# Modulation batches placed behind the next group of small matmuls, with a shorter gap to their loads and other metering of the convolution taps

## The chip, the cores and the metric

The kernel runs on one core of a Trainium2 chip. The core has a matrix engine (TensorE, PE in the rows, its weight loads PEld), a vector engine (VectorE, DVE), a scalar engine (ScalarE, ACT), GpSimd (POOL) and SyncE (SP), which here issues most DMAs. Each engine works through its own list of instructions in order; semaphores tie the lists together. The metric is the time of one execution in microseconds, the median of several runs.

## The reference

One layer of a hybrid backbone, over 128 context tokens and 256 latent tokens with 2048 channels, all float32:

```python
sh1, sc1, g1, sh2, sc2, g2 = modulation(cond, lp["w_mod"], lp["b_mod"])   # silu(cond) @ w_mod + b_mod
hcur = x * (1 + sc1) + sh1
q, k, v, u, gt, z, xbc, dt = jnp.split(hcur @ lp["w_in"], cuts, axis=-1)
o_a = attention(q, k, v)                  # 16 heads; latent: neighbourhood plus context keys
o_b = conformer_conv(u, gt, ...)          # silu(LN(dwconv31(u * sigmoid(gt))))
o_c, h_state = ssd_mixer(z, xbc, dt, ...) # dwconv5, chunked scan in both directions, gate, RMSNorm
mix = jnp.concatenate([o_a, o_b, o_c], axis=-1) @ lp["w_out"]
x = layer_norm(ALPHA * x + g1 * mix, ...)
hcur = x * (1 + sc2) + sh2
ff = conv_ffn(hcur, lp["w_up"], ..., lp["w_down"])
x = layer_norm(ALPHA * x + g2 * ff, ...)
```

The six modulation vectors are products of a 2048-vector (two of them: context and latent) with a 2048 x 12288 matrix. Four of the six belong to the stage that the change touches or lie near it: gate 1 and scale 2 are made on TensorE ("modulation batches" below), shift 2 on VectorE.

## The kernel before

**Large matmuls.** A float32 weight piece is loaded (`wpiece`), ScalarE rounds it to a high part `whi` (line 229) and VectorE subtracts to get the low part `wlo` (line 230, "weight split"). Each product is three matmuls, high by high, high by low and low by high: lines 454 to 456 (`tok_mm`, tokens on the output partitions) and 460 to 462 (`chan_mm`, channels on the output partitions). There are four `whi` and four `wlo` buffers of half a piece each.

**The stage.** After the first input projection comes a stage with a hand-made order on TensorE: line 993 opens a `manual_schedule` for that engine alone, so TensorE's list is the order in which the code emits; the lists of the other engines are set by a scheduler from program order, priorities and its own estimates. The large matmuls of the stage are, in order: z and dt (`phase_zd`), values (`phase_v`), eight head pairs of keys and queries (`qk_tile`), and the first 512 output columns (`wo_group(0, ...)`).

**The planner.** Between them, groups of small matmuls are put in by a planner, `_Flow`. It keeps a clock in estimated microseconds. `tick(us)` is called after each few large matmuls and moves the clock; generators that are due are then run up to their next `yield cost, delay`: the clock moves by `cost` and the generator comes back `delay` later. The generators of the stage are:
- `tok_gen`: transposes of the convolved channels (lines 418, 424);
- `dt_gen`: the time steps of the scan. Line 498 makes two cumulative sums, line 499 copies each to `cs` on VectorE, lines 501 and 503 go on from there;
- `ssm_gen`: the scan (lines 541, 579, 584, 592, transposes on 608);
- `attn_gen`: per head pair and block of queries, scores (lines 698, 701, 703), then one step later the transposes of the softmax (line 726) and a step later the values (line 739), copied by line 742;
- `conv_ln_gen`: the LayerNorm of the 31-wide convolution (lines 372, 385), once the convolution is done;
- `mod2_gen`: the modulation batches. 64 pieces, three at a time (`most`), in 22 batches, each followed by its `gap`. A batch loads three pieces of 128 x 1024 floats (512 KB each, `mod2_load`) into the three `v` buffers, waits `gap` on the planner's clock, and then makes four matmuls of 32 columns of weights for each piece (line 786). They are `gm<-v,cond` in the rows: `cond` is loaded as weights in 32-column tiles, `v` streams through;
- `sh2_gen`: the products for shift 2 on VectorE.

The 31 taps of the convolution (line 358, and 354 for the first of a channel tile; 124 in all) are the planner's background `bg`: `tick` adds `us * rate` to a credit and emits taps while the credit lasts. `rate` is 0.45 up to the end of `phase_v` and 0.7 from then on. The taps run on VectorE.

Of the kernel before, what the change touches and what calls it, by code (L numbers as in the profile page):

```python
# [47 lines left out]
class _Flow:  # L48
# [2 lines left out]

    def __init__(self, step):
        self.now, self.last, self.n, self.q, self.bg, self.credit, self.step = 0.0, 0.0, 0, [], [], 0.0, step
        self.rate = 0.0

    def add(self, delay, gen):
        self.n += 1
# [2 lines left out]
    def run(self):  # L60
        self.last = self.now
        while self.q and self.q[0][0] <= self.now:
            gen = heappop(self.q)[2]
            said = next(gen, None)
            if said is not None:
                self.now += said[0]
                self.add(said[1], gen)

    def tick(self, us):
        self.now += us  # L70
# [12 lines left out]
    def drain(self):  # L83
        while self.bg:
            self.bg.pop(0)[0]()
        while self.q:
            self.advance()


# [10 lines left out]
def _build(tc, ctx, a):  # L100
# [16 lines left out]
    flow = _Flow(1.5)  # L117
# [232 lines left out]
    def conv31_steps(i):  # L350
        def first():
            do_glu(i)
            cvo[i] = t_t(399)
            V.tensor_scalar(out=cvo[i][:, :399], in0=glu[i][:, 0:399], scalar1=P_("conv_w", 31 * i),
                            scalar2=P_("conv_b", i), op0=ALU.mult, op1=ALU.add)

        def tap(j):
            V.scalar_tensor_tensor(out=cvo[i][:, :399], in0=glu[i][:, j:j + 399], scalar=P_("conv_w", 31 * i + j),
                                   in1=cvo[i][:, :399], op0=ALU.mult, op1=ALU.add)

        return [(first, 1.2)] + [(lambda j=j: tap(j), 0.63) for j in range(1, 31)]
# [3 lines left out]
    def conv_ln_gen():  # L365
        while flow.bg:
            yield 0.0, 1.0
        yield 0.0, 3.0
        n = 399
        ps = at_t()  # L370
        for i in range(4):
            PE.matmul(ps[:, :n], ones, cvo[i][:, :n], start=i == 0, stop=i == 3)
        mu = g_t()
        S.activation(out=mu[:, :n], in_=ps[:, :n], func=AF.Copy, scale=1.0 / 512)
        yield 2.7, 3.0
        sqs = []
        for i in range(4):
            V.tensor_tensor(out=cvo[i][:, :n], in0=cvo[i][:, :n], in1=mu[:, :n], op=ALU.subtract)
            sq = g_t()
            S.activation(out=sq[:, :n], in_=cvo[i][:, :n], func=AF.Square)  # L380
            sqs.append(sq)
            yield 0.0, 2.0
        sm = at_t()
        for i in range(4):
            PE.matmul(sm[:, :n], ones, sqs[i][:, :n], start=i == 0, stop=i == 3)
        rs = g_t()
        S.activation(out=rs[:, :n], in_=sm[:, :n], func=AF.Sqrt, scale=1.0 / 512, bias=eps_t)
        yield 2.7, 0.0
        for c0, c1 in ((0, 133), (133, 266), (266, 399)):
            yield 0.0, 3.0  # L390
            V.reciprocal(out=rs[:, c0:c1], in_=rs[:, c0:c1])
        for i in range(4):
            yield 0.0, 2.0
            V.tensor_tensor(out=cvo[i][:, :n], in0=cvo[i][:, :n], in1=rs[:, :n], op=ALU.mult)
        for i in range(4):
            for c0, c1 in CSEG:
                S.activation(out=cvo[i][:, c0:c1], in_=cvo[i][:, c0:c1], func=AF.Silu,
                             scale=P_("cln_g", i), bias=P_("cln_b", i))
            ready.add(8 + i)
# [8 lines left out]
    def do_conv5(i):  # L408
        o = t_t(386)
        taps(o, xbc_raw[i], lambda j: ("sconv_w", 5 * i + j), 5, P_("sconv_b", i), 386)  # L410
        S.activation(out=o, in_=o, func=AF.Silu)
        xact[i] = o

    def tok_gen():
        for c in range(3):
            ps = at_t()
            for i in range(4):
                PE.transpose(ps[:, 128 * i:128 * i + 128], xact[i][:, OFF[c]:OFF[c] + 128], ident)
            xtok[c] = m_t()
            S.copy(out=xtok[c], in_=ps)  # L420
            yield 0.5, 1.5
            ps = at_t()
            for i in range(2):
                PE.transpose(ps[:, 128 * i:128 * i + 128], xact[4 + i][:, OFF[c]:OFF[c] + 128], ident)
            btok[c] = sbt([128, 256], "btok", 3)
            S.copy(out=btok[c], in_=ps[:, :256])
            yield 0.3, 1.5
        ready.add("tok")
# [187 lines left out]
    def ssm_gen():  # L616
        while not {"tok", "dt"} <= ready:
            yield 0.0, 1.0
        yield from state_steps(0, 0)
        yield from state_steps(0, 1)  # L620
        yield from chunk_steps(0)
        load_state()
        yield from state_steps(1, 0)
        yield from state_steps(2, 1)
        yield from chunk_steps(1)
        yield from chunk_steps(2)
        ready.add("ssm")
        ready.update(range(12, 16))
# [147 lines left out]
    def mod2_start(g):  # L776
        gS[g] = gm_t()

    def mod2_load(i):
        g, half, k = i // 32, i // 16 % 2, i % 16  # L780
        return load(a["wm2"][g, half, k], 1024, v_t().rearrange("p a b -> p (a b)"))

    def mod2_piece(i, raw):
        g, half, k = i // 32, i // 16 % 2, i % 16
        for j in range(4):
            PE.matmul(gS[g][32 * j:32 * j + 32, 256 * half:256 * half + 256], cond[:, k, :],
                      raw[:, 256 * j:256 * j + 256], start=k == 0, stop=k == KC - 1)
# [5 lines left out]
    def mod2_end(g):  # L793
        ps = gS.pop(g)
        vv = v_t()
        sm, bg = vv[:, 0, :], vv[:, 1, :]
        if g == 0:
            pinned(bg, a["bgate"])
            with tc.high_priority(offset=HP):
                V.tensor_tensor(out=sm, in0=ps, in1=bg, op=ALU.add)  # L800
            gd[g] = dr.tile([2, D], F32, tag=f"gd{g}", name=nm("gd"))
            for j in range(4):
                G.dma_start(out=gd[g][:, 512 * j:512 * j + 512], in_=sm[32 * j:32 * j + 2, :])
            return
        V.tensor_copy(out=sm, in_=ps)
        yield 0.0, 2.0
        pt = at_t()
        for b in range(4):
            PE.transpose(pt[:, 128 * b:128 * b + 128], sm[:, 128 * b:128 * b + 128], ident)
        pv = pt.rearrange("p (b j c) -> p j b c", b=4, j=4)[:, :, :, 0:2]  # L810
        V.tensor_tensor(out=s2.rearrange("p (j b) c -> p j b c", j=4), in0=pv,
                        in1=bc(b2p.rearrange("p (j b) -> p j b", j=4), 3, 2), op=ALU.add)
        yield 0.5, 1.0

    def mod2_gen(most, gap):
        i = 0
        while i < 64:
            n = min(most, 32 - i % 32)
            raws = [mod2_load(j) for j in range(i, i + n)]
            yield 0.0, gap  # L820
            if i % 32 == 0:
                mod2_start(i // 32)
            for j, raw in enumerate(raws):
                mod2_piece(i + j, raw)
            i += n
            yield 0.45 + 0.43 * n, 0.0
            if i % 32 == 0:
                yield from mod2_end((i - 1) // 32)
# [52 lines left out]
    def sh2_gen(gap):  # L881
        while "ssm" not in ready:
            yield 0.0, 1.0
        for _ in range(3):
            sh2_load()
            yield 0.0, gap
        while "stop" not in ready:
            sh2_step()
            yield 0.0, gap
# [103 lines left out]
    with tc.manual_schedule(engines={mybir.EngineType.PE}):  # L993
        for i in range(8):
            do_conv5(i)
        for i in range(4):
            flow.bg += conv31_steps(i)
        flow.rate = 0.45
        flow.add(30.0, tok_gen())
        flow.add(0.0, mod2_gen(3, 12.0))  # L1000
        flow.add(40.0, conv_ln_gen())
        flow.add(30.0, ssm_gen())
        flow.add(50.0, attn_gen())
        flow.add(60.0, sh2_gen(4.0))
        phase_zd()
        flow.add(0.0, dt_gen())
        phase_v()
        flow.rate = 0.7
        for hp in range(8):
            k = qk_tile(0, hp)  # L1010
            qk[hp] = (qk_tile(1, hp), k)
        ps = [mm_t() for _ in range(3)]
        for k in ORDER[:12]:
            cat_split(k)
        wo_group(0, ps, cat_split, lambda last: flow.tick(2.09))
        ready.add("stop")
        flow.drain()
        gb = mix_rows(0)
        for t in range(3):
            mix_evac(t, 0, 0, 512, ps[t], gb)  # L1020
# [333 lines left out]
```

## Time and profile before

| | us |
|---|---|
| median of 3 runs | 1811.7 (1810.92 to 1812.44) |
| the profiled execution | 1812.03 |
| its span, first to last instruction | 1810.2 |
| TensorE busy | 1780.8 (98%) |
| VectorE busy | 1213.4 (67%) |
| ScalarE busy | 774.6 (43%) |

The page tells the busy time of each engine, and the trace behind it each instruction with its start, its duration and what it waited for. On TensorE the starts are what counts: matmuls overlap at their ends, so the distance between two starts is the time that a matmul costs. In the order of time, a row ends with idle time in brackets where the engine stood still before it, and the name of what ended that.

### The profile page before, as it was taken

The numbers are of one execution on the slowest core, as the hardware profiler recorded it, in microseconds if no ns is written. First come the engines' busy times: TensorE is split into PE (matmuls) and PEld (weight loads), VectorE is DVE, ScalarE is ACT, GpSimd is POOL, SyncE is SP. The second block draws the span as 40 slices with busy tenths as digits, with TensorE's granted clock in tenths as the row PEclk, the third lists the DMA queues.
The fourth block names the chain that finished last, engine by engine and source line by source line (L and its number), as shares of the span: only waits on it lengthen the run. The fifth ranks groups of instructions, "written<-read, shape, count | busy, mean of one in ns | idle before, by whom it ended". The sixth has DMA issues, their size and how long they took to land. (4 is left out here: it accounts for less than half of the span.)

```text
span 1810.2 us, 28844 instructions
## 1 busy us (share of the span) xinstructions
PE 1780.8 (98%) x10794; PEld 1620.9 (90%) x10794; DVE 1213.4 (67%) x2591; ACT 774.6 (43%) x1466; POOL 62.6 (3%) x149
## 2 busy tenths in 40 slices
PE   7999999999999999999999999999999999999998
PEld 6888997888887899999889999989999988999987
DVE  3866899885999566667535667535676544766577
ACT  4222454656764246444433444323444323444434
POOL 0000001110001000000000000000000000000000
PEclk9999999999999999999999999999999999999999
DMA  8999457766999452445444454444544544444454
GB/s 317 310 322 321 148 199 254 241 210 204 356 344 336 138 162 86 142 140 161 130 129 152 151 175 162 135 128 134 175 163 145 158 123 140 163 146 153 121 152 139
DMA packets 113259, 337.75 MB, mean 187 GB/s; under 512 B 13096, under 2 KB 17672, under 8 KB 113120
## 3 DMA queue, kind: packets, MB, share of 16 engines
q1 hardware_dynamic: 105888, 311.65, 52.2%
q0 software_dynamic: 7232, 24.28, 4.5%
q8 instruction: 84, 1.38, 0.3%
q14 instruction: 55, 0.45, 0.1%
HBM read 331.08 MB, written 4.79 MB: 186 GB/s over the span
## 5 line engine op out<-in xcount | busy, mean ns | idle before, releaser
L229 ACT CAST whi<-raw 128x512 fp32r<-128x512 f32 (+1 forms) x755 | 467.5, 620 | 869.1 <-PE mm L461 291.4
L230 DVE TENSOR_TENSOR wlo<-raw,whi 128x512 fp32r<-128x512 f32 (+1 forms) x755 | 519.8, 689 | 428.3 <-ACT whi L229 426.4
L460 PE MATMUL mm<-hl,whi 128*128 128x384 f32 x1245 | 425.2, 342 | 1.4 <-ACT whi L229 1.1
L461 PE MATMUL mm<-hl,whi 128*128 128x384 f32 x1245 | 419.5, 337 | 0.0
L462 PE MATMUL mm<-hl,wlo 128*128 128x384 f32 x1245 | 418.8, 336 | 0.0
L460 PEld LDWEIGHTS mm<-hl,whi 128*128 128x128 f32 x1245 | 233.6, 188 | 12.2 <-issue 5.5
L461 PEld LDWEIGHTS mm<-hl,whi 128*128 128x128 f32 x1245 | 233.8, 188 | 0.6 <-DVE wlo L230 0.2
L462 PEld LDWEIGHTS mm<-hl,wlo 128*128 128x128 f32 x1245 | 233.7, 188 | 0.0
L460 PE MATMUL sc<-hl,whi 128*128 128x384 f32 x659 | 222.8, 338 | 0.0
L461 PE MATMUL sc<-hl,whi 128*128 128x384 f32 x659 | 221.8, 337 | 0.0
L462 PE MATMUL sc<-hl,wlo 128*128 128x384 f32 x659 | 221.7, 336 | 0.0
L460 PEld LDWEIGHTS sc<-hl,whi 128*128 128x128 f32 x659 | 123.6, 188 | 2.9 <-ACT whi L229 1.6
L461 PEld LDWEIGHTS sc<-hl,whi 128*128 128x128 f32 x659 | 123.7, 188 | 0.1
L462 PEld LDWEIGHTS sc<-hl,wlo 128*128 128x128 f32 x659 | 123.7, 188 | 0.0
L843 DVE SCALAR_TENSOR_TENSOR junk<-raw,gb 128x512 bf16<-128x512 f32 x128 | 87.6, 684 | 51.1 <-DMA raw<-wg 50.9
L454 PE MATMUL mm<-whi,hl 128*128 128x512 f32 (+2 forms) x293 | 101.2, 345 | 0.1
L456 PE MATMUL mm<-whi,hl 128*128 128x512 f32 (+2 forms) x293 | 99.4, 339 | 0.0
L455 PE MATMUL mm<-wlo,hl 128*128 128x512 f32 (+2 forms) x293 | 99.3, 339 | 0.0
L456 PE MATMUL mm<-whi,t 128*128 128x512 f32 (+1 forms) x232 | 89.6, 386 | 0.0
L454 PE MATMUL mm<-whi,t 128*128 128x512 f32 (+1 forms) x232 | 89.6, 386 | 0.0
L843 DVE SCALAR_TENSOR_TENSOR junk<-m,m 128x512 bf16<-128x512 f32 x128 | 87.9, 687 | 2.5 <-DMA m<-wsh 0.6
L455 PE MATMUL mm<-wlo,t 128*128 128x512 f32 (+1 forms) x232 | 89.5, 386 | 0.0
(353 smaller groups left out, 2474.8 us busy)
## 6 DMA issues: line engine op xcount, KB each, us to landing
raw<-wu SPq DMA_DIRECT2D x176, 512.0 KB, 3.5
raw<-wd SPq DMA_DIRECT2D x79, 512.0 KB, 3.6
m<-wm SPq DMA_DIRECT2D x128, 256.0 KB, 5.7
v<-wm SPq DMA_DIRECT2D x64, 512.0 KB, 6.4
raw<-wA SPq DMA_DIRECT2D x32, 512.0 KB, 5.4
raw<-wqk SPq DMA_DIRECT2D x32, 512.0 KB, 4.5
m<-wsh SPq DMA_DIRECT2D x64, 256.0 KB, 6.1
raw<-wo SPq DMA_DIRECT2D x32, 512.0 KB, 4.7
```

The source lines that it names most:

```text
L229: S.copy(out=hi[:, :w], in_=rw)
L230: V.tensor_tensor(out=lo[:, :w], in0=rw, in1=hi[:, :w].bitcast(F32), op=ALU.subtract)
L454: PE.matmul(ps[:, :n], A, hi[:, w0:w0 + n], start=k == 0, stop=False)
L455: PE.matmul(ps[:, :n], A, lo[:, w0:w0 + n], start=False, stop=False)
L456: PE.matmul(ps[:, :n], B, hi[:, w0:w0 + n], start=False, stop=k == last)
L460: PE.matmul(ps[:, :T], A, hh[k], start=k == k0, stop=False)
L461: PE.matmul(ps[:, :T], A, hl[k], start=False, stop=False)
L462: PE.matmul(ps[:, :T], B, hh[k], start=False, stop=k == k1)
L843: V.scalar_tensor_tensor(out=j, in0=w, scalar=1.0, in1=cbc[s], op0=ALU.mult, op1=ALU.mult, accum_out=macc[:, 16 * s + kt, kq:kq + 1])
```

## The change

Three things. (1) A generator may now say `None` as its delay. Then it is put on a list `behind`, and is run as soon as another generator has emitted a group with a cost above zero. `mod2_gen` says so once, after its gap, so that a batch's matmuls stand directly behind the next group of small matmuls in TensorE's list. `drain` empties the list at the end of the stage. (2) The gap between a batch's loads and its matmuls is 5 instead of 12 on the planner's clock. (3) The rate of the taps is 0.25 instead of 0.45 up to the end of `phase_v`, and 0.85 instead of 0.7 after it. No matmul, load or vector instruction is added or dropped.

```diff
--- before.py
+++ after.py
@@ -51,7 +51,7 @@
 
     def __init__(self, step):
         self.now, self.last, self.n, self.q, self.bg, self.credit, self.step = 0.0, 0.0, 0, [], [], 0.0, step
-        self.rate = 0.0
+        self.rate, self.behind = 0.0, []
 
     def add(self, delay, gen):
         self.n += 1
@@ -64,7 +64,14 @@
             said = next(gen, None)
             if said is not None:
                 self.now += said[0]
-                self.add(said[1], gen)
+                if said[1] is None:
+                    self.behind.append(gen)
+                else:
+                    self.add(said[1], gen)
+                if said[0] > 0:
+                    for other in self.behind:
+                        self.add(-1.0, other)
+                    self.behind = []
 
     def tick(self, us):
         self.now += us
@@ -83,7 +90,9 @@
     def drain(self):
         while self.bg:
             self.bg.pop(0)[0]()
-        while self.q:
+        while self.q or self.behind:
+            while self.behind:
+                self.add(0.0, self.behind.pop())
             self.advance()
 
 
@@ -818,6 +827,7 @@
             n = min(most, 32 - i % 32)
             raws = [mod2_load(j) for j in range(i, i + n)]
             yield 0.0, gap
+            yield 0.0, None
             if i % 32 == 0:
                 mod2_start(i // 32)
             for j, raw in enumerate(raws):
@@ -995,9 +1005,9 @@
             do_conv5(i)
         for i in range(4):
             flow.bg += conv31_steps(i)
-        flow.rate = 0.45
+        flow.rate = 0.25
         flow.add(30.0, tok_gen())
-        flow.add(0.0, mod2_gen(3, 12.0))
+        flow.add(0.0, mod2_gen(3, 5.0))
         flow.add(40.0, conv_ln_gen())
         flow.add(30.0, ssm_gen())
         flow.add(50.0, attn_gen())
@@ -1005,7 +1015,7 @@
         phase_zd()
         flow.add(0.0, dt_gen())
         phase_v()
-        flow.rate = 0.7
+        flow.rate = 0.85
         for hp in range(8):
             k = qk_tile(0, hp)
             qk[hp] = (qk_tile(1, hp), k)
```

Lines behind the class move by 9 in the changed kernel, and by 10 behind `mod2_gen`'s new line: line 786 is 795 there, 499 is 508, 742 is 751.

TensorE, values (`phase_v`): the two cumulative sums of the time steps (`at<-dA`) and what stands around them. Before:

```order
L456 MATMUL mm_3087<-whi_3245,hl_87 128x512
L498 MATMUL at_3263<-dA_95,cons_66 128x24 x2
L454 MATMUL sc_3085<-whi_3249,hl_86 128x512
L455 MATMUL sc_3085<-wlo_3250,hl_86 128x512
L456 MATMUL sc_3085<-whi_3249,hl_87 128x512
```

and in the changed kernel:

```order
L465 MATMUL mm_3057<-whi_3204,hl_87 128x512
L507 MATMUL at_3222<-dA_95,cons_66 128x24 x2
L795 MATMUL gm_2967<-v_3122,cond_63 32x256 x4
L795 MATMUL gm_2967<-v_3124,cond_63 32x256 x4
L795 MATMUL gm_2967<-v_3126,cond_63 32x256 x4
L463 MATMUL sc_3055<-whi_3208,hl_86 128x512
L464 MATMUL sc_3055<-wlo_3209,hl_86 128x512
L465 MATMUL sc_3055<-whi_3208,hl_87 128x512
```

A batch of three pieces now stands between the cumulative sums and the nine large matmuls that come before line 501 (510); before there were the nine alone.

VectorE, the same place: from the first copy of `cs` to just behind the second. `wlo` is a weight split, `t<-g,par,t` a tap, `vt` the addition of a finished group of values. Before:

```order
L499 COPY cs_89<-at_3263 128x3x8
L358 SCALAR_TENSOR_TENSOR t_3231<-g_3225,par_68,t_3231 128x399
L230 TENSOR_TENSOR wlo_3359<-raw_3356,whi_3358 128x512
L667 TENSOR_TENSOR vt_326<-vt_326,sc_3085 128x512
L667 TENSOR_TENSOR vt_327<-vt_327,sc_3086 128x512
L667 TENSOR_TENSOR vt_328<-vt_328,mm_3087 128x512
L230 TENSOR_TENSOR wlo_3363<-raw_3356,whi_3362 128x512
L499 COPY cs_89<-at_3263 128x3x8
```

and in the changed kernel:

```order
L508 COPY cs_89<-at_3222 128x3x8
L367 SCALAR_TENSOR_TENSOR t_3500<-g_3494,par_68,t_3500 128x399
L239 TENSOR_TENSOR wlo_3310<-raw_3307,whi_3309 128x512
L508 COPY cs_89<-at_3222 128x3x8
L367 SCALAR_TENSOR_TENSOR t_3500<-g_3494,par_68,t_3500 128x399
```

The second copy now comes ahead of the three additions and of one of the two splits.

ScalarE, values of the sixth head pair: `t<-at` is the copy of line 742 (751), `hl<-t` the rounding of a finished input of the output projection, `qk<-mm` a finished query tile. Before:

```order
L245 CAST hl_6126<-t_3699 128x128
L229 CAST whi_6166<-raw_6164 128x512
L245 CAST hl_6126<-t_3231 128x256
L245 CAST hl_6126<-t_3699 128x256
L245 CAST hl_6126<-t_4296 128x256
L245 CAST hl_6126<-t_2632 128x256
L742 COPY t_5977<-at_5962 128x384
L728 COPY pt_5981<-at_5979 128x128
```

and in the changed kernel:

```order
L725 ACTIVATE p_5864<-p_5864,sm_5863 128x128
L238 CAST whi_5940<-raw_5934 128x512
L238 CAST whi_6021<-raw_6019 128x512
L238 CAST whi_6025<-raw_6019 128x512
L691 COPY qk_5930<-mm_5797 128x384
L751 COPY t_5962<-at_5947 128x384
L737 COPY pt_5966<-at_5964 128x128
```

The roundings of `hl` no longer stand ahead of the copy.

## Rows read from the trace of the kernel before

**Rows 1.** The page, part 1: busy time of the engines, share, instructions.

```profile
PE 1780.8 (98%) x10794; PEld 1620.9 (90%) x10794; DVE 1213.4 (67%) x2591; ACT 774.6 (43%) x1466; POOL 62.6 (3%) x149
```

**Rows 2.** Stretches: us; PE, PEld, DVE, ACT, POOL busy (instructions), clock, DMA.

```profile
260.00:290.00 30.00, 27.98 (x182) 22.03 (x180) 29.81 (x69) 14.51 (x28) 0.51 (x1) 1.00 0.60 205
290.00:330.00 40.00, 40.00 (x249) 34.62 (x241) 39.43 (x68) 15.85 (x35) 7.24 (x12) 1.00 0.79 272
330.00:380.00 50.00, 47.43 (x364) 41.05 (x364) 36.34 (x80) 31.25 (x81) 6.18 (x10) 1.00 0.62 211
380.00:430.00 50.00, 49.22 (x369) 42.11 (x370) 37.76 (x80) 35.27 (x90) 9.80 (x16) 1.00 0.70 229
```

**Rows 3.** TensorE's waits for others: total us, times, longest.

```profile
PE at L726 <- ACT t L742: 3.9, 7, 1.1
```

**Rows 4.** TensorE in order of time: a batch alone. Start, us, instruction.

```profile
478.21 0.33 PE L461 MATMUL mm<-hl,whi 128*128 128x384 f32 x1
478.38 0.34 PE L462 MATMUL mm<-hl,wlo 128*128 128x384 f32 x1
478.65 1.50 PE L786 MATMUL gm<-v,cond 128*32 128x256 f32 x24
480.09 0.44 PE L460 MATMUL mm<-hl,whi 128*128 128x384 f32 x1
480.37 0.34 PE L461 MATMUL mm<-hl,whi 128*128 128x384 f32 x1
```

**Rows 5.** TensorE: scores ahead of a large matmul, and ahead of a batch.

```profile
483.05 0.49 PE L698 MATMUL sc<-qk,qk 64*128 64x128 f32 x4
483.47 0.44 PE L460 MATMUL mm<-hl,whi 128*128 128x384 f32 x1
...
330.06 0.49 PE L698 MATMUL sc<-qk,qk 64*128 64x128 f32 x4
330.48 1.50 PE L786 MATMUL gm<-v,cond 128*32 128x256 f32 x24
```

**Rows 6.** TensorE: line 584 ahead of a large matmul, and ahead of a batch.

```profile
328.03 1.00 PE L584 MATMUL at<-m,m 128*128 128x64 f32 x8
328.84 0.42 PE L460 MATMUL mm<-hl,whi 128*128 128x384 f32 x1
...
377.48 1.00 PE L584 MATMUL at<-m,m 128*128 128x64 f32 x8
378.41 1.50 PE L786 MATMUL gm<-v,cond 128*32 128x256 f32 x24
```

**Rows 7.** TensorE: waits of small matmuls in order of time.

```profile
286.22 0.42 PE L501 MATMUL at<-dA,cons 128*128 128x48 f32 x2 [1.53 <-DVE cs L499]
...
338.42 0.33 PE L726 MATMUL at<-cons,p 128*128 128x128 f32 x1 [0.89 <-ACT p L716]
...
438.16 0.52 PE L726 MATMUL at<-cons,p 128*128 128x128 f32 x3 [0.43 <-DVE m L595]
...
492.81 0.33 PE L726 MATMUL at<-cons,p 128*128 128x128 f32 x1 [0.32 <-ACT t L742]
...
520.40 0.33 PE L726 MATMUL at<-cons,p 128*128 128x128 f32 x1 [0.99 <-ACT t L742]
```

**Rows 8.** ScalarE in order of time, ahead of the copy of line 742.

```profile
518.65 1.32 ACT L245 CAST hl<-t 128x256 fp32r<-128x256 f32 x4
519.88 0.47 ACT L742 COPY t<-at 128x384 f32<-128x384 f32 x1
```

**Rows 9.** DMA issues of 256 to 259 and 509 to 512 us: KB, us to landing.

```profile
v<-wm SPq DMA_DIRECT2D x3, 512.0 KB, 6.1
...
v<-wm SPq DMA_DIRECT2D x3, 512.0 KB, 10.0
```

**Rows 10.** Groups by line on VectorE: weight split and tap; busy us, mean ns.

```profile
L230 DVE TENSOR_TENSOR wlo<-raw,whi 128x512 fp32r<-128x512 f32 (+1 forms) x755 | 519.8, 689 | 428.3 <-ACT whi L229 426.4
...
L358 DVE SCALAR_TENSOR_TENSOR t<-g,par,t 128x399 f32<-128x399 f32 x120 | 74.9, 639 | 0.7
```

## The prediction

> **What bounds the kernel now.** I read the page's busy shares first: TensorE is busy for 1780.8 us, 98% of the span [rows 1]. So a change can only give back what lies between TensorE's matmuls, or lose by opening new holes. Next come the stretches of the stage that the change reorders, about 240 to 575 us [rows 2]. TensorE's idle time there is the stretch less its busy time: 2.0 us in 260 to 290, none in 290 to 330, 2.6 in 330 to 380, 0.8 in 380 to 430. In the same rows VectorE is full in the first two (29.8 of 30, 39.4 of 40) and has room in the next two (36.3 and 37.8 of 50, so 25.9 us free). The granted clock is 1.00 in all four, and the change makes no long hole, so I give the clock nothing.
>
> The third view is the order of time on TensorE. The large matmuls of the weights (lines 454 to 462) follow each other without holes. Time is lost where a group of small matmuls stands between them, in two ways: the switch itself, and a small matmul that waits for VectorE or ScalarE.
>
> **The price of a switch, from the rows.** A modulation batch (line 786, twelve matmuls) that stands alone: the last large matmul starts at 478.38, the second one behind the batch at 480.37, 1.99 us later. Two large ones at 0.17 (478.21 to 478.38) leave 1.65 us. The batch to the next large matmul is 1.44 of it (478.65 to 480.09) [rows 4]. So 0.21 us is entry and exit.
>
> Behind a pair of scores (line 698) the entry is free: scores to large matmul takes 0.42 us (483.05 to 483.47), scores to batch 0.42 too (330.06 to 330.48) [rows 5]. The exit is paid by the scores anyway. Such a batch adds 1.44 and saves 0.21 against standing alone.
>
> Behind a group that uses the whole array it is less: line 584 to a large matmul takes 0.81 us (328.03 to 328.84), line 584 to a batch 0.93 (377.48 to 378.41) [rows 6]. Such a batch adds 1.56 and saves 0.09.
>
> The rows of 6 against those of 5 say that what stands ahead matters. The Trainium skill, TensorEngine Tiling (Array Packing), section Tiling Modes, has a rule for it: changing the tiling mode, not just the tile, drains TensorE. The batch works in 32-column tiles, and lines 418, 498, 541, 579, 584 and 608 on the full array, so by that rule a batch behind those still pays both drains and saves nothing, and only the batches behind scores or values save. By that rule the placement is worth 4 x 0.21 = 0.8 us; if every place were as good as that behind scores it would be 14 x 0.21 = 2.9 us.
>
> **Part 1, the placement.** Of the 22 batches, counted in the order of TensorE, 15 have a large matmul ahead of them before the change, 3 a full-array group, 4 scores or values. Afterwards it is 1, 13 and 8. So 14 batches leave the dear place, 10 of them for the full-array place and 4 for that behind scores: 10 x 0.09 + 4 x 0.21 = 1.7 us gained. The bounds are 0.8 (full-array places worth nothing) and 2.9 (all at 0.21). Groups other than these batches are also run together (41 stretches of small work hold them instead of 46). Rows 6 show no clear gain for full-array groups, so I give it nothing; its upper bound is 5 x 0.21 = 1.0 us.
>
> **Part 2, the waits that go.** Four waits of TensorE have a visible reason in the order of before that is gone after [rows 7].
> First, line 501 waits 1.53 us for the second copy of cs (line 499) on VectorE. Between the two copies stand one tap, two weight splits and three adds of line 667. After the change one tap and one split stand there, 0.64 + 0.69 = 1.3 us [rows 10], and on TensorE a batch of 1.44 us stands behind line 498, so the copy should be done well ahead. Gain 1.5.
> Second, the first transposes of the attention (line 726 at 338.42) wait 0.89 us for the softmax, while VectorE is full. After, VectorE's order holds no tap instead of 18 between the 115th and the 127th weight split, and TensorE has the four matmuls of line 584 more ahead of the transposes. Gain 0.9.
> Third, at 438.16 transposes wait 0.43 us for line 595, which reads the same pair of PSUM buffers. After, no transposes stand directly behind line 592; the 14 matmuls of line 739 come first or a large matmul does. Gain 0.4.
> Fourth, at 520.40 the wait for the copy of line 742 is 0.99 us where it is 0.32 elsewhere (492.81): casts of line 245 stand ahead of the copy on ScalarE, and the copy begins only at 519.88 [rows 8]. After, three weight casts and the copy of a query stand there, as ahead of 492.81. Gain 0.99 - 0.32 = 0.7.
> Sum 3.5 us. The other waits for line 742 (3.9 us in all [rows 3]) stay: each group of values is still followed at once by transposes. The bounds are 1.5 (only the first goes, the rest turn up at other groups) and 3.5.
>
> **Part 3, what is new.** (a) Loads. A batch needs three loads of 512 KB into three buffers, and the third buffer is free when the batch before has ended, 1.44 us after its start. Of three loads the middle one lands 6.1 us after its issue in one row and 10.0 in another [rows 9]. The third piece is used two thirds of 1.44 us, 0.96, into the next batch. So two batches must start 6.6 to 10.5 us apart. The planner's gap falls from 12 to 5 us, but the wait for a group comes on top, and the order shows 22 batches over nearly the same stretch. Most stand 30 to 70 large matmuls apart; four follow after 12 to 45 with few groups between. The closest has 24 large matmuls (4.1), the batch before (1.44), twice line 584 (0.81 each) and a pair of scores (0.42) between: 7.6 us. It waits 0 by the first landing and 2.9 by the second; the four together 0 to 11.6. TensorE is in order, so a batch that waits holds the weight matmuls behind it. The row of 6.1 is from 256 us, that of 10.0 from 509; the four close batches stand before 430, so the first is nearer and I take 0.5 us.
> (b) Taps. The metering (rate 0.45 to 0.25, then 0.7 to 0.85) moves 31 taps past the 128th weight split (31 stand behind it before, 62 after). At 0.639 us each [rows 10] that is 19.8 us of VectorE in 330 to 430, which has 25.9 free [rows 2]. It fits, with 6 us to spare; a softmax step can now meet a running tap. From 0 to 5 x 0.64 = 3.2 us, one running tap at each of the five softmax steps of that stretch; I take 0.3. The cover is the 30 or more large matmuls between scores and their transposes (5.1 us); at one place it is 24 with a batch and a group between. The conv LayerNorm, which waits for the last tap, comes 6 large matmuls later, and nothing waits for it before the output projection.
> Sum 0.8 us. The last batch moves behind the end of the first output group; what needs it (line 809) still stands nine large matmuls behind it, so I change nothing there.
>
> **Sum.** 1.7 + 3.5 - 0.8 = 4.4 us. The profiled execution took 1812.03 us (span 1810.2, and 1.8 around it), 0.3 above the median of 1811.7. I take the gain from the median: 1807.3 us, 0.24% less. Faster or slower by over 0.2% (3.6 us, about what a measurement of this kernel can tell from no change) means below 1808.1 or above 1815.3.
>
> **Rivals.** First, the waits move instead of going: only the one at line 501 goes, and transposes wait for other VectorE work (the taps now lie under the attention). For it speaks that VectorE is left 6 us free; against it that no tap stands at the first softmax and that the casts of the fourth are gone from the order. 1.7 + 1.5 - 0.8 = 2.4 us, 1809.3, no change.
> Second, the placement does less than it says: the 0.09 us of rows 6 is one pair of places and may be nothing, so that only the four batches behind scores save, and of the waits only the first goes. 0.8 + 1.5 - 0.8 = 1.5 us, 1810.2, no change. The rule on tiling modes in the Trainium skill (TensorEngine Tiling (Array Packing), Tiling Modes) would have it so.
> Third, the loads do not land in time: the four close batches wait 2.9 us each, 11.6 us. The point is a landing of about 7 us for the closest one, and 10 for all four. 1811.7 - 5.2 + 11.6 + 0.3 = 1818.4, slower. Against it speak the landings of 6 us and that the queue of loads shows the batch's loads right behind its predecessor, not behind a weight load that waits.
>
> **How the numbers follow.** The forecast 0.55, the first rival 0.28, the second 0.11, the third 0.06. Faster 0.55, same 0.39, slower 0.06. The forecast alone spans 1804.5 to 1808.1: by the upper bounds of placement it is 1.2 us lower, of merged groups 1.0 and without new waits 0.8. The range of all cases goes up over both rivals of no change and leaves out the third: 1804.3 to 1811.3.
>
> **What would show it.** A batch behind scores: 0.42 from scores to batch, as here; behind full-array groups about 0.93 after line 584. The wait at line 501 (510 after) gone; the first transposes without a wait; no idle time at line 786 that ends with a load. If idle time at that line appears at the four close batches, the third rival; if the waits list has new entries of transposes for VectorE or for the p of line 716 between 340 and 430 us, the first.

## The result, and the profile after

The changed kernel takes 1823.4 us (median of 4 runs, 1822.55 to 1825.85) where the kernel before, beside it, takes 1811.3 (1809.7 to 1812.44): ratio 1.0065, 95% interval 1.0053 to 1.0078. It is slower by 12 us; the forecast was 4 us faster, and the range ended at 1811.3. The profiled execution has a span of 1820.8 us, 10.6 more than before. Line numbers below are those of the changed kernel, 9 or 10 above those of before.

The page of the changed kernel, part 1, answers to [rows 1]:

```profile
PE 1786.4 (98%) x10794; PEld 1624.3 (89%) x10794; DVE 1216.6 (67%) x2591; ACT 773.8 (43%) x1465; POOL 63.0 (3%) x149
```

TensorE is busy 5.6 us longer with the same instructions, so they ran slower somewhere. Stretches of the changed kernel, the columns of [rows 2] (the number behind POOL's instructions is the granted clock):

```profile
330.00:380.00 50.00, 46.67 (x315) 41.01 (x313) 41.89 (x86) 30.89 (x76) 6.50 (x10) 0.93 0.58 195
380.00:430.00 50.00, 47.72 (x383) 41.45 (x383) 42.59 (x90) 31.32 (x83) 9.34 (x16) 1.00 0.63 211
530.00:580.00 50.00, 44.94 (x299) 33.50 (x300) 46.76 (x138) 27.41 (x66) 7.37 (x14) 0.90 0.85 293
360.00:370.00 10.00, 10.00 (x79) 8.26 (x71) 7.58 (x16) 2.63 (x9) 0.00 (x0) 0.81 0.62 211
530.00:540.00 10.00, 5.26 (x34) 3.18 (x38) 9.47 (x28) 6.40 (x17) 0.54 (x1) 0.55 0.56 178
```

Two stretches of the stage have a clock below 1.00, 330 to 380 and 530 to 580. What TensorE waited for in the changed kernel (total us, times, longest), which answers to [rows 3]:

```profile
PE at L735 <- ACT p L725: 6.1, 3, 4.7
...
PE at L735 <- ACT pt L737: 3.0, 1, 3.0
PE at L735 <- ACT t L751: 2.6, 7, 0.7
...
PE gm L795 <- DMA v<-wm: 0.7, 2, 0.6
```

The waits for the copy of line 751 fell from 3.9 to 2.6 us in all, more than the 0.7 that was forecast, and the batches hardly wait for loads. The wait of the first line was 1.1 us in all before, and that of the second is new.

**The first stall, 354 to 363 us.** TensorE in order of time:

```profile
353.98 0.49 PE L735 MATMUL at<-cons,p 128*128 128x128 f32 x3
357.48 0.90 PE L735 MATMUL at<-cons,p 128*128 128x128 f32 x3 [3.01 <-ACT pt L737]
...
359.04 2.79 PE L795 MATMUL gm<-v,cond 128*32 128x256 f32 x24
361.76 0.69 PE L469 MATMUL mm<-hl,whi 128*128 128x384 f32 x1
```

The second transposes wait for the copy of the first (the scan, the transposes and the values share two PSUM buffers, `at` in the kernel). ScalarE in the same stretch:

```profile
354.47 0.60 ACT L238 CAST whi<-raw 128x512 fp32r<-128x512 f32 x1
356.66 0.40 ACT L572 ACTIVATE m<-m,ncs 128x128 f32<-128x128 f32 x1 [1.59 <-POOL m L569]
356.97 0.46 ACT L737 COPY pt<-at 128x384 f32<-128x384 f32 x1
```

And GpSimd, which it waits for:

```profile
352.42 0.56 POOL L567 DMA_DIRECT2D m<-csd  x1
355.87 0.75 POOL L569 TENSOR_SCALAR_AFFINE_SELECT m<-m 128x512 f32<-128x512 f32 x1 [2.90 <-DMA m<-csd]
```

ScalarE is free from about 355, and the copy could run. But an exponential of the scan's decays (line 572) stands ahead of it in ScalarE's list; that waits for GpSimd's select, and the select for a DMA issued only at 352.42. TensorE's wait ends with a DMA's landing, three lists away. Behind it the batch takes 2.72 us (359.04 to 361.76) where it took 1.44 [rows 4]: the lower of the two clock levels, 1.2 instead of 2.4 GHz.

**The second stall, 528 to 541 us.** TensorE in order of time:

```profile
528.51 0.34 PE L471 MATMUL mm<-hl,wlo 128*128 128x384 f32 x1
533.59 0.90 PE L735 MATMUL at<-cons,p 128*128 128x128 f32 x3 [4.74 <-ACT p L725]
535.64 0.90 PE L735 MATMUL at<-cons,p 128*128 128x128 f32 x3 [1.15 <-ACT p L725]
...
538.06 2.79 PE L795 MATMUL gm<-v,cond 128*32 128x256 f32 x24
540.78 0.68 PE L469 MATMUL mm<-hl,whi 128*128 128x384 f32 x1
```

ScalarE in the same stretch:

```profile
525.47 0.58 ACT L722 ACTIVATE p<-sc,sm 128x384 f32<-128x384 f32 x1 [4.21 <-DVE sm L718]
526.04 0.89 ACT L254 CAST hl<-t 128x128 fp32r<-128x128 f32 x4
...
527.35 2.67 ACT L254 CAST hl<-t 128x256 fp32r<-128x256 f32 x7
...
530.44 2.06 ACT L254 CAST hl<-t 128x384 fp32r<-128x384 f32 x5
...
532.92 0.61 ACT L725 ACTIVATE p<-p,sm 128x384 f32<-128x384 f32 x1
```

The softmax begins late (line 718 on VectorE stands behind shift-2 products), and between its exponential and its scaling sixteen casts of line 254 run, for the first output columns. They have the highest priority and stand where the scheduler's estimate finds them ready. Before the change they were spread over 517 to 533 us in groups of two and four; those of [rows 8] are one of these groups.

**What they cost.** Take as the cost of a group the distance between the large matmuls around it, less their own pace. The group at 353.12 costs 8.95 us; its two halves cost 3.96 without a wait in the kernel `both` below; 0.7 more goes into slow large matmuls behind it: 5.7 us. The group at 533.59 costs 12.40, one of the same kind at 474.64 costs 3.14: 9.3 us. Of these 15.0 us, 8.9 are idle time (3.01 + 4.74 + 1.15); the remaining 6.1 I put down to the lower clock. 10.6 - 15.0 = -4.4: the rest of this one execution is 4.4 us shorter than that of before, the figure that the forecast summed. By the medians, 12.1 us apart, it would be 2.9, and the parts do not agree one by one (below), so the match is in part luck.

### The profile page after: what moved, and what is told of

The parts are those of the page before. It is cut to its first block, busy times and chain, and to the rows that moved or that the text cites. A ratio compares the mean times of both kernels' runs of the same rounds, so it can differ in the third digit from the quotient of the medians.

```text
span 1820.8 us, 28844 instructions
## 1 busy us (share of the span) xinstructions
PE 1786.4 (98%) x10794; PEld 1624.3 (89%) x10794; DVE 1216.6 (67%) x2591; ACT 773.8 (43%) x1465; POOL 63.0 (3%) x149
```

## The experiments

The theory at the start: two accidental stalls, and a placement that gains 4 to 5 us. The rivals: batches behind groups cost time by themselves; the moved taps cost it.

**The parts alone and in pairs.** Placement is the planner's edit with `yield 0.0, None`; the others are numbers:

```diff
place_only:   mod2_gen(3, 5.0) -> mod2_gen(3, 12.0); rates 0.25, 0.85 -> 0.45, 0.7
place_gap:    rates 0.25, 0.85 -> 0.45, 0.7
place_rates:  mod2_gen(3, 5.0) -> mod2_gen(3, 12.0)
rates_only:   (before) rates 0.45, 0.7 -> 0.25, 0.85
gap_only:     (before) mod2_gen(3, 12.0) -> mod2_gen(3, 5.0)
```

> The placement alone (gap 12, rates 0.45 and 0.7 as before). Theory: the changed kernel pays for two accidental stalls, one of about 6 us at 357 us (the scan's exponentials of line 572 stand in ScalarE's list ahead of the copy of line 737 and wait for a DMA) and one of about 9 us at 530 us (some sixteen casts of line 254 stand ahead of a softmax scaling, line 725), while the placement itself gains 4 to 5 us. In the list of this kernel on ScalarE the casts stand behind both scalings of their pair and no waiting exponential stands directly ahead of those copies, so I expect 1807, from 1804.5 to 1810. First rival, that batches behind groups cost time by themselves (longer stretches of small work): 1815 or more. Second rival, that the taps moved under the attention are what costs: 1807 here too, and the cost in the kernel with the rates alone.

> The two new rates alone (0.25 and 0.85), no placement, gap 12. Theory of the two stalls: on ScalarE eight casts stand between the two scalings of one pair (part of the stall at 530 us, 0 to 4 us), and no waiting exponential ahead of the copies: 1811 to 1816, most likely 1813. First rival (the placement costs): 1811, no change. Second rival (the moved taps cost, 31 of them at 0.6 us on VectorE): 1818 or more, with waits of transposes for VectorE between 340 and 430 us.

> Placement and the gap of 5, the rates as before. Theory of the two stalls: on ScalarE all four exponentials of the scan's second decays stand ahead of the two copies of line 737 at the place of the first stall, as in the changed kernel, and twelve casts stand ahead of two copies, fourteen ahead of the next exponential of a softmax: both stalls show in some size, 1813 to 1822. First rival (the placement costs): about 1820, with the time spread over the groups. Second rival (the taps cost): 1807, since the rates are those of before.

> Placement and the new rates, the gap 12 as before. Theory of the two stalls: on ScalarE no waiting exponential stands directly ahead of the copies at 357 us, so that the first stall is gone; eighteen casts stand ahead of one pair's exponentials and scalings, so that the second is there: 1807 plus 4 to 9 us, 1811 to 1816. First rival (the placement costs): 1818 to 1823. Second rival (the taps cost): 1820 or more, with waits for VectorE between 340 and 430 us. If the short gap (loads closer to their use) were the cause, this one would be at 1807.

Measured: `place_only` 1832.2 (ratio 1.0114, 1.0099 to 1.0129), `rates_only` 1813.2 (1.0011, 1.0001 to 1.0020), `place_gap` 1822.2 (1.0058, 1.0043 to 1.0074), `place_rates` 1837.8 (1.0148, 1.0133 to 1.0164). Placement alone missed its expectation by 25 us. TensorE behind the end of the first output columns in `place_only`:

```profile
587.88 1.08 PE L795 MATMUL gm<-v,cond 128*32 128x256 f32 x8 [9.33 <-DMA v<-wm]
```

This is the first of fourteen single pieces between 587 and 618 us. A batch that waits for a group after a gap of 12 comes so late that the batches do not fit into the stage; the rest is emitted at the end and runs at the pace of its loads. Those groups cost 24 us; the groups ahead of 584 us cost 4.5 less than before, but hold fourteen pieces of 0.43 us, 6.0 us, less. `place_rates` has the same tail (18 us) and a wait of 6.3 us at the casts (there the scaling waits for line 724 on VectorE, which stands behind the low parts of the casts, line 255). So the short gap is no tuning beside the placement but a condition of it. The taps are not the cause: the rates alone cost about 2 us (0.2 to 3.6), and `place_gap`, with the old rates, is as slow as the changed kernel. But its waits are others. TensorE stands still at the first place for VectorE instead of ScalarE:

```profile
358.75 0.87 PE L735 MATMUL at<-cons,p 128*128 128x128 f32 x3 [4.00 <-DVE m L558]
```

Its waits for scalings (line 725) are 2.0 us in all, where the changed kernel has 6.1. So the two stalls above belong to the changed kernel; another order with these batches is as slow by other waits.

> The kernel before with the gap of 5 instead of 12 and nothing else. The placement alone ran its batches so late that thirteen pieces (of 64) were left at the end of the stage and waited there for their loads (24 us in groups behind 584 us). By that, the gap of 5 is not there to save time but to make room for the wait for a group, and alone it should only bring the batches earlier. All batches have loads that land in 6 to 10 us, and here they can follow 5 us plus 1.4 behind one another: if loads bind (the third rival of the prediction), idle time ahead of line 786 that ends with a DMA, and 1815 to 1820. If they do not: 1809 to 1813. On ScalarE twelve casts stand ahead of two copies of line 728, which may cost up to 3 us. I expect 1812.

`gap_only`: 1828.2 (1.0094, 1.0077 to 1.0111). TensorE's largest wait there (total us, times, longest):

```profile
PE gm L786 <- DMA v<-wm: 9.8, 9, 4.8
```

Without the wait for a group the batches follow each other as closely as the gap allows, and the loads do not land: the third rival's mechanism, in another kernel. These waits are 9.8 of its 17 us; the rest is not followed here. In the changed kernel the groups keep them apart (0.7 us).

**The stalls taken away.** `cast_late` gives the casts no priority, `turn_wait` moves one attention step, `both` does both:

```diff
# cast_late, in cat_split
-        with tc.high_priority(offset=HP):
+        with tc.high_priority(offset=0):
# turn_wait, in attn_gen
+                if (hp, blk) == (1, 0): yield 0.0, 3.0
                 if p:
...
-                yield cost, 6.5 if hp < 7 else 5.0
+                yield cost, 3.5 if (hp, blk) == (1, 0) else 6.5 if hp < 7 else 5.0
```

> The changed kernel with the casts of line 254 (and 255) at the priority of their place in the program instead of ahead of everything. TensorE's order up to 618 us is that of the changed kernel. On ScalarE one cast instead of sixteen then stands between an exponential (line 722) and its scaling (line 725) of the sixth pair. Theory of the two stalls: the idle time of 4.7 and 1.2 us ahead of line 735 at 530 us goes, and with it the lower clock behind it, 9 us in all, and the first stall stays: 1823.4 - 9.4 = 1814, from 1812 to 1816.5. Rival, that the order of these casts only moves the wait (the first output columns, line 463 at 542 us, or the transposes then wait for casts): 1820 or more.

> The changed kernel with one attention step 3 us later on the planner's clock (the transposes that stalled at 357 us; the step behind it is 3 us earlier again), so that twelve large matmuls stand between line 550 and these transposes. Theory: the first stall (3.0 us of idle time and some 3 us of slower matmuls behind it) goes. The lists of the other engines move too: at the second place both scalings of the pair now stand ahead of the casts, and twelve casts ahead of the two copies of the next transposes. By the first stall alone 1817; with the second smaller by 5 to 9 us, 1808 to 1812. I expect 1811, from 1807 to 1817.5. Rival, that the longer stretches of small matmuls cost the time, not these two waits: 1820 or more.

> Both edits on the changed kernel: the step 3 us later, and the casts at their own priority. Theory of the two stalls: both waits go and what is left is the gain of placement and of the waits that the change removed: 1808, from 1805.5 to 1811.5. Rival (the waits move on, or longer stretches of small matmuls cost the time): 1816 or more.

Measured: `cast_late` 1819.4 (1.0042, 1.0027 to 1.0057), `turn_wait` 1815.1 (1.0019, 1.0009 to 1.0028), `both` 1811.9 (1.0004, 0.9995 to 1.0014). The transposes of the second stall no longer wait in `cast_late`, but the first output columns do, five microseconds later:

```profile
538.96 0.80 PE L463 MATMUL mm<-whi,hl 128*128 128x512 f32 x1 [4.05 <-ACT hl L254]
```

The matmuls behind it are slow again, and more than half of that stall came back there: what the rival described, if not quite its 1820. In `both` the two stalls are gone, the clock is 1.00 at both places, and 11.5 us of the 12.1 are back. But the forecast gain does not show in the time. Its waits:

```profile
PE at L735 <- ACT t L751: 3.5, 7, 1.6
...
PE mm L465 <- DVE hl L255: 1.8, 1, 1.8
...
PE at L735 <- ACT p L725: 1.2, 1, 1.2
...
PE gm L796 <- DMA v<-wm: 1.0, 1, 1.0
PE at L735 <- DVE m L558: 0.8, 1, 0.8
```

**Fewer shift-2 products, as intended.** Four kernels ask for one shift-2 step in 6 us of the planner's clock instead of 4: `sh2` is the changed kernel with that, `both_sh2`, `tw_sh2` (with `turn_wait`) and `before_sh2` the others.

```diff
-        flow.add(60.0, sh2_gen(4.0))
+        flow.add(60.0, sh2_gen(6.0))
...
-        ... lambda last: sh2_step() if cg < 3 else None)
+        ... lambda last: [sh2_step() for _ in range(2 if sh2_n[0] % 4 == 0 else 1)] if cg < 3 else None)
```

> The changed kernel with a third fewer shift-2 products (line 853, VectorE) in the stage: one step each 6 us of the planner's clock instead of 4, made up in the output groups behind it. The lists of TensorE and ScalarE in the stage stay as in the changed kernel, casts included. At the second stall VectorE ran seven such products (0.73 us each) ahead of line 718, so that ScalarE waited 4.2 us for it, and then sixteen casts stood ahead of the scaling. If both make the stall: it shrinks by 3 to 6 us with the slower matmuls behind it, the first stall stays, 1818, from 1815.5 to 1820.5. If the casts on ScalarE alone set it: 1822 or more.

> The kernel with both edits (a step 3 us later, casts at their own priority), and the same third fewer shift-2 products in the stage. With both edits the time was that of the kernel before (1811.9), with waits left that end with VectorE or with work queued behind it: 1.8 us for a low part of a cast (line 255), 1.2 for a scaling, 0.8 for line 558. If VectorE's load between 480 and 580 us (49 of 50 us) is what eats the gain, these 3 us go: 1809, from 1807 to 1811. If the waits move on again: 1811 to 1814.

> The kernel with the step 3 us later alone (casts ahead of everything, as in the changed kernel), and a third fewer shift-2 products. Without the second edit it took 1815.1. It also gives the trace that shows the place of the first stall with casts as in the changed kernel: there no idle time over 1 us ahead of line 735 between 350 and 362 us, and a granted clock of 1.00 in that stretch. Theory: 1812, from 1809 to 1815.

> The control: the kernel before with a third fewer shift-2 products and nothing of the change. Its waits that could shrink are 0.99 us for a copy of line 742 and about 1 us for scalings, so 1810.5, from 1808.5 to 1812. If it gains as much as the kernel with both edits, that gain is none of the change's.

Measured: 1823.3 (1.0059, 1.0046 to 1.0073), 1812.5 (1.0001, 0.9992 to 1.0010), 1814.5 (1.0013, 1.0004 to 1.0022) and 1812.6 (1.0004, 0.9996 to 1.0013). None gained, and none of the four is a test of VectorE's load: the edit hardly changed what VectorE does. Up to 580 us it starts 111 products in `sh2` and 114 in the changed kernel, 111 in `both_sh2` and 111 in `both`, 120 in `before_sh2` and 121 before. At the second stall `sh2` has the same 4.21 us of ScalarE waiting for line 718 behind the same train of products. How much of the second stall VectorE makes stays open. The trace of `tw_sh2` serves to read `turn_wait`'s edit. The first stall is gone there (no idle time over 0.82 us ahead of line 735 at that place, clock 1.00), but so is the second: the longest wait between 520 and 550 us is 1.43 us, the clock 1.00. One edit moved the lists at both places, so the 8.3 us between the changed kernel and `turn_wait` are no price of the first stall alone.

**Softmax first.** The order of the lists is changed and not the amount of work: lines 718 to 725 and the copies of lines 737 and 751 get the priority of the casts. In the traces TensorE's groups stand in the same order as in the kernel it is applied to.

```diff
# in scores, around lines 718 to 725; in turned and values around the copy
+            with tc.high_priority(offset=HP):
# before_cs and before_cs_soft, around the copy of line 499 of before
+            with tc.high_priority(offset=HP): V.tensor_copy(out=csv[:, :, d_, :], ...)
```

> The changed kernel with the softmax steps (lines 718, 722, 724, 725) and the copies of lines 737 and 751 at the same high priority as the casts, on VectorE and ScalarE. TensorE's list stays that of the changed kernel, except two rows near the end of the stage. On ScalarE one small cast instead of sixteen casts then stands between an exponential and its scaling of the pair of the second stall; at the first stall the exponentials of line 572 still stand ahead of the copies. Theory of the two stalls: the second goes without a new wait for casts, 1823.4 - 9.4 = 1814, from 1811.5 to 1816. Rival (the casts only come later, and the first output columns wait for them, as with the casts at their own priority, 1819.4): 1818 or more.

> The same, and the step 3 us later that took the first stall away. Both stalls are gone here without holding the casts back. If nothing but these lists ate the gain, what is left is the gain that the prediction summed, less the placement's part that the rows do not show (batches behind full-array groups cost 1.62 to 1.63 us, as alone): 1808.5, from 1806.5 to 1811. If the waits that the change takes away come back at other places whatever the priorities: 1810 to 1814.

> The control: the kernel before with the same steps at high priority, and nothing of the change. TensorE's list is that of the kernel before. Its waits for scalings and copies (0.99 us at 520 us, 0.89 at 338 us, some smaller ones) can shrink by 1 to 2 us: 1810, from 1808 to 1812. What it gains is no gain of the change.

> The kernel before with only the copies of line 499 ahead of everything on VectorE. TensorE's list is that of the kernel before. This is the first of the prediction's waits (1.53 us ahead of line 501) by itself: on VectorE one tap instead of one tap, two splits and three additions stands between the two copies. If the 1.5 us are on the path that sets the end: 1810.0, from 1808.5 to 1811. If the time is given back at the next wait: 1811 to 1812.5.

`after_soft`: 1818.9 (1.0039, 1.0025 to 1.0053). The second stall at line 735 is gone and, as in `cast_late`, the output columns wait now:

```profile
538.41 0.50 PE L465 MATMUL mm<-whi,hl 128*128 128x512 f32 x1 [2.57 <-DVE hl L255]
```

So in the changed order the sixteen casts are late for somebody either way: for the transposes if they go first, for the output columns if they go behind. `tw_soft` (no stall at line 735, softmax first) takes 1812.2 (1.0001, 0.9992 to 1.0010), `before_soft` 1811.3 (0.9996, 0.9987 to 1.0005). The changed order with these edits is no faster than the order before with the same priorities. In `tw_soft` too the output columns wait, 3.35 us in three pieces:

```profile
531.47 0.49 PE L463 MATMUL mm<-whi,hl 128*128 128x512 f32 x1 [0.83 <-ACT hl L254]
...
533.22 0.50 PE L465 MATMUL mm<-whi,hl 128*128 128x512 f32 x1 [1.03 <-DVE hl L255]
535.21 0.50 PE L463 MATMUL mm<-whi,hl 128*128 128x512 f32 x1 [1.49 <-ACT qk L689]
```

Here the clock falls as well, to 0.83 in 530 to 540 us.

`before_cs`: 1810.6 (0.9992, 0.9983 to 1.0001). The first wait of [rows 7] by itself is gone:

```profile
285.08 0.32 PE L501 MATMUL at<-dA,cons 128*128 128x48 f32 x2
```

The point estimate is 1.3 us, near the 1.5 of the row, with an interval that just reaches no change.

> The kernel before with both priority edits (the copies of line 499, and the softmax steps with the copies of lines 728 and 742), nothing of the change, TensorE's list as before. Alone the first gave 0.9992 and the second 0.9996 of the time before. If waits that are taken away on an unchanged TensorE list add up: 0.9988, that is 1809.6, from 1808.5 to 1811. If they are given back at the next wait: 1811 to 1812.

`before_cs_soft`: 1809.2 beside 1812.4 for before, ratio 0.9985, 0.9975 to 0.9994. Without anything of the change under test it is 0.15% faster than the kernel before, and the interval excludes no change. The size agrees with two removals that add up on an unchanged TensorE list (0.08% and 0.04% by themselves, neither of them clear of no change).

## Why the prediction was wrong

**Part 1, the placement: right in kind, too large.** Two pairs of the changed kernel, without waits. TensorE, line 550 with a batch behind it and without, and scores (line 707) with and without:

```profile
291.04 1.03 PE L550 MATMUL at<-m,btok 128*128 128x256 f32 x4
292.00 1.50 PE L795 MATMUL gm<-v,cond 128*32 128x256 f32 x24
...
293.77 0.40 PE L464 MATMUL mm<-wlo,hl 128*128 128x512 f32 x1
...
297.70 1.03 PE L550 MATMUL at<-m,btok 128*128 128x256 f32 x4
...
298.80 0.40 PE L464 MATMUL mm<-wlo,hl 128*128 128x512 f32 x1
...
511.00 0.49 PE L707 MATMUL sc<-qk,qk 64*128 64x128 f32 x4
511.42 1.50 PE L795 MATMUL gm<-v,cond 128*32 128x256 f32 x24
...
513.13 0.34 PE L470 MATMUL mm<-hl,whi 128*128 128x384 f32 x1
...
456.18 0.49 PE L707 MATMUL sc<-qk,qk 64*128 64x128 f32 x4
...
456.88 0.33 PE L470 MATMUL mm<-hl,whi 128*128 128x384 f32 x1
```

From the group's start to the second large matmul: 2.73 less 1.10, so a batch adds 1.63 behind the full-array group, as good as the 1.65 alone [rows 4]; 2.13 less 0.70, so 1.43 behind scores. The saving is 0.02 and 0.22, not 0.09 and 0.21. If all go by these pairs, the ten batches that went behind full-array groups gained 10 x 0.02, the four behind scores 4 x 0.22: 1.1 us, where 1.7 was taken. The term was mis-sized by reading [rows 6], an entry only, where entry and exit were wanted. The rule that was weighed there (the Trainium skill, TensorEngine Tiling (Array Packing), Tiling Modes) put it at 0.8 by giving full-array places nothing; the 1.63 us of this trace agree with it.

**Part 2, the waits that go: right, with one not listed.** All four went. TensorE at the three places with rows of their own:

```profile
284.51 0.32 PE L510 MATMUL at<-dA,cons 128*128 128x48 f32 x2
...
334.65 0.38 PE L735 MATMUL at<-cons,p 128*128 128x128 f32 x2
...
520.63 0.33 PE L735 MATMUL at<-cons,p 128*128 128x128 f32 x1 [0.32 <-ACT t L751]
```

They answer to the first, second and last of [rows 7]. The fourth was counted as gone because the casts of [rows 8] no longer stood ahead of that copy. They had not left the list: they stood a little further on, ahead of a scaling that the next transposes wait for. I looked at where rows had been, and not at where they went. And one wait of before was on no list of mine, the second transposes directly behind line 541, 1.36 us:

```profile
349.61 0.52 PE L726 MATMUL at<-cons,p 128*128 128x128 f32 x3 [1.36 <-DVE m L549]
```

It went too, a gain that I had not counted. But transposes directly behind the same line (550) are where the first stall of the changed kernel and the 4.00 us of `place_gap` stand, so the kind of place was on record.

**Part 3, what is new: this is the step that failed.** It listed two things, loads and taps, and took 0.8 us for all that is new; the runs show 15.0 us in its place. The two that it listed were small: 0.7 us of waits for loads, and no transposes behind taps. But the groups of the whole stage moved against the lists of the other engines, and the scheduler orders those anew by its own estimates. The two waits that decided stood behind an exponential with its select and its DMA, and behind casts, and neither was looked for. The first rival named the mechanism (waits move instead of going) and let it give back only what was gained: its price had no room for a wait of 4.7 us, nor for a place beyond 430 us.

**The clock.** "The change makes no long hole, so I give the clock nothing" rested on the holes I had listed. With the stalls came some 6.1 us at the lower level, two thirds of their idle time again.

**The forecast itself.** Without the two stalls the trace is 4.4 us shorter than before, as summed, but no kernel had that time, and the sum came out by errors that offset each other: the placement gave 1.1 and not 1.7, and waits went that were not counted. `both` and `tw_soft` took the stalls away and ended at 1.0004 and 1.0001. By the measure used above, the groups of the stage cost 118.0 us in the trace of before, 115.8 in that of `both` and 114.3 in that of `tw_soft`. So 2.2 and 3.7 us were gained among the groups, and about as much went into the waits of the first output columns (2.1 and 3.35 us, in `tw_soft` with the lower clock behind them). This is read from single executions. What is shown is that each way of removing the stalls brought waits of 1 to 4 us elsewhere; that any order with these batches must do so is not shown.

## What to carry to other kernels

When one engine's list is reordered, read the lists of all the others at every place where that engine waits: what stands between a producer and the rows ahead of it, down to the DMA, and follow a row that left a place to its new one. Change parts that condition each other only together: here the wait for a group needs the short gap, and the short gap needs the wait. What gained here was moving producers forward while the busiest engine's list stayed as it was: small gains, 0.15% for two of them together.

## What the runs showed of the hardware that I had not expected

A wait of TensorE cost more than its length. Behind 3.01 us of idle time a batch took 2.72 us instead of 1.44, and so it did behind the holes of 4.74 and 1.15; the granted clock was 0.81 in 360 to 370 us, where before it was 1.00. Behind a hole of 1.82 us in `both` it stayed at 1.00 (530 to 540 us). And a batch in 32-column tiles costs the same behind a full-array group as alone (1.63 and 1.65 us) but 0.22 less behind scores.
